# Decoder trunk on one core: sample keys fetched one sample ahead and multiplied on VectorE, the samples' cross scores moved into the first feed-forward

## The chip, the cores and the metric

The kernel runs on one core of a Trainium2 chip. The metric is the device time of one execution in microseconds, from the first to the last instruction with what the launch adds around them. Three runs of the kernel before took 3188.86, 3189.97 and 3193.72 us; their median is 3189.97 us.

## What is computed

One layer of a decoder trunk in float32, for two groups at once: a prompt of 2048 tokens and 8 samples of one token each (model width 1024).

1. Normalise, project to pool, q, k and v; a pooling mixer for one half of the width, differential attention (4 heads, two score maps of 64 dimensions each) for the other half; output projection, added to x.
2. Normalise, cross-attention (4 heads of 256) into 256 memory tokens, added to x.
3. Normalise, feed-forward 1024 to 2 x 2816 with a causal convolution of width 3, silu gate, down to 1024, added to x. Final norm.

The samples attend to caches in place of the prompt. Two pieces of the reference are computed by the lines that change:

```python
# differential attention of a sample: 512 cached keys, found through a page table of 4 pages of 128 rows
past_k = cache_k[l][page_table].reshape(Bs, -1, N_DIFF_HEADS, 2 * DIFF_HD)
s = jnp.einsum('bqhcd,bkhcd->bhcqk', q, k) * (DIFF_HD ** -0.5)
# cross-attention of a sample: its own 256 memory keys, 4 heads of 256
s = jnp.einsum('bqhd,bkhd->bhqk', q, mem_k) * (CROSS_HD ** -0.5)
```

## The kernel before, in words

The prompt is cut into four chunks of 512 tokens, features on the partitions; the 8 sample tokens ride as 8 extra columns of chunk 3. Every product of the prompt is a float32 product made of three matmuls: weight and activation are split into a rounded part (hi, a copy on ScalarE) and a remainder (lo, a subtraction on VectorE), and lo x hi, hi x hi and hi x lo are summed. `split` (L88) and `mm3` (L92) do it for activations, the class `Weight` (L281) for weights: stage 0 loads 512 KB by the SP queue (L291), stage 1 casts `whi` on ScalarE (L294), stage 2 subtracts `wlo` on VectorE (L297).

The order of all work is one list written by hand (L1658 to L1679) that `drive` (L396) walks; each item issues instructions to the engines' in-order queues. An item has a cost (TensorE's share of it) and a latency. `weave(main, extra, lo, hi)` (L337) spreads the items of `extra` by their latencies over the stretch from `lo` to `hi` of the costs of `main`. `look(4, 3, 2)` (L391) lets raw weights run four, casts three and remainders two weights ahead of use. `later(dt, ...)` (L373) holds an epilogue back by so many units of cost.

Tiles come from rings: `H` has 43 buffers of 1060 columns, shared by weights, activations and sample data; `St` has 6 buffers of 536 columns; PSUM has four banks in `PB` and two double banks in `PA`. A transfer into a ring's buffer waits, in its queue, until the last reader of the buffer's old content is done, and what stands behind it in that queue waits too. The SP queue carries the loads of weights and activations and the broadcasts of the samples' queries; the POOL queue carries stores (`ST = G`) and the gathers through the page table.

Two stretches hold what changes.

*First stretch, "stage A"* (L1672): the cross-attention scores of chunk 1 (`sc_[1]`: four heads, matmuls L94 to L96 into S, softmax L1220 to L1228, turned by L1248 into `Ahi`, `Alo`), then the output projection of chunk 2 (`wo[2]`: an item `load` that fetches x and mix and splits mix into `mixhi` and `mixlo`, then eight projections L443). The samples' first attention is woven in from 0 to 0.95: `sample_index`, `sample_rows` (writes the queries to `qs_d`), eight `sample_scores(b)` (L865), `sample_softmax`, `sample_weights`. One `sample_scores(b)` loads the query to all partitions (`qb`, an `St` buffer, SP queue), then twice: two gathers of 128 rows x 512 (L872, POOL queue) into one `kg`, the product kg x qb on GpSimd (L877), and sums over 64 on VectorE (L879) with scale and bias (four small L882 a sample).

*Second stretch, "stage B"* (L1675): the scores of chunk 3 (`sc_[3]`), then its value product (`vo[3]`, L94 to L96 into `vo`). Woven in from 0.3 to 0.95: the list `sc_items`, then `n3[0]`, the feed-forward's norm of chunk 0. `sc_items` is the samples' cross query (`both("q", ...)`, four items of two weights each, L1320), its write to `qcs_d`, eight `sc_scores(b)` (L1344), `sc_softmax`, `sc_weights`. One `sc_scores(b)` broadcasts the query (`qcb`, 512 KB, SP queue), then twice: loads 512 KB of memory keys (`cmk`, L1350), multiplies on GpSimd (L1351), sums over 256 on VectorE (L1352). 

Behind it stands the feed-forward of chunk 0 (`ffn_items(0)`, L1628: 44 up-projections `up`, L429 and L432, of cost 5.3; 88 pieces of the down-projection `down`, L1503, of cost 1.3), with `sc_items2` (the samples' cross values and their output projection) and `n3[1]` woven in. Three more feed-forwards follow, and the final norm.

Of the kernel before, what the change touches and what calls it, by code (L numbers as in the profile page):

```python
# [15 lines left out]
ALU = mybir.AluOpType  # L16
# [4 lines left out]
P = 128  # L21
T = 2048
NS = 8
D = 1024
# [17 lines left out]
PAGES = 4  # L42
# [4 lines left out]
def tile_trunk_step(ctx: ExitStack, tc: tile.TileContext, a, o):  # L47
    nc = tc.nc
    V, S, G, PE, SY = nc.vector, nc.scalar, nc.gpsimd, nc.tensor, nc.sync
# [10 lines left out]
    def H(name, dt=F32):  # L60
        return hp.tile([P, HT], dt, tag="H", name=name)

    def St(name, dt=F32):
        return sp.tile([P, SW], dt, tag="S", name=name)
# [10 lines left out]
    def v3(t, k, n=None):  # L75
        n = n if n is not None else 1024 // k
        return t[:, : k * n].rearrange("p (k n) -> p k n", k=k)
# [7 lines left out]
    def bc(ap, shape, axis):  # L85
        return ap.unsqueeze(axis).broadcast_to(shape)
# [229 lines left out]
    def item(specs, fn, cost=0.0, lat=0.0):  # L316


        return (specs, fn, cost, max(lat, cost, 0.3))
# [17 lines left out]
    def weave(main, extra, lo=0.0, hi=1.0):  # L337

        tm, te = sum(i[2] for i in main) or 1.0, sum(i[3] for i in extra) or 1.0
        out, k, dm, de = [], 0, 0.0, 0.0  # L340
        for i in main:
            out.append(i)
            dm += i[2]
            while k < len(extra) and lo + (hi - lo) * (de / te) <= dm / tm:
                out.append(extra[k])
                de += extra[k][3]
                k += 1
        return out + extra[k:]
# [42 lines left out]
    def look(*n):  # L391
        def fn(_):
            ahead[:] = n
        return item([], fn)
# [455 lines left out]
    idx = cp.tile([P, NS * PAGES], I32, name="idx")  # L850
# [11 lines left out]
        G.memset(coef[0:32], 1.0)  # L862
        V.tensor_copy(coef[32:64], lamv[32:64, 1:2])

    def sample_scores(b):  # L865
        def fn(_):
            qb = St("qb")
            SY.dma_start(qb[:, :512], qs_d[b].partition_broadcast(P))
            for pp in range(2):
                kg = H("kg")  # L870
                for j in range(2):
                    G.indirect_dma_start(  # L872
                        out=kg[:, j * 512:(j + 1) * 512], out_offset=None,
                        in_=a["cache_k"].rearrange("o n s h d -> (o n s) (h d)"),
                        in_offset=bass.IndirectOffsetOnAxis(ap=idx[:, b * PAGES + 2 * pp + j:b * PAGES + 2 * pp + j + 1],
                                                            axis=0))
                G.tensor_tensor(v3(kg, 2), v3(kg, 2), bc(qb[:, :512], [P, 2, 512], 1), ALU.mult)  # L877
                r = St("sr")
                V.tensor_reduce(v3(r, 16, 1), kg[:, :1024].rearrange("p (a d) -> p a d", d=HD), AX.X, ALU.add)  # L879
                r4 = r[:, :16].rearrange("p (g h c) -> p g h c", g=2, h=NH)  # L880
                for c in range(2):
                    V.scalar_tensor_tensor(sal[:, 2 * pp:2 * pp + 2, c, b, :], r4[:, :, :, c], 0.125,  # L882
                                           sbias[:, 2 * pp:2 * pp + 2, :], ALU.mult, ALU.add)
        return fn

    sbias = cp.tile([P, PAGES, NH], F32, name="sbias")

# [104 lines left out]
                     t1.rearrange("p (h b) -> p h b", h=NH))  # L992

    sample_items = [item([], sample_index), item([], sample_rows, 2.0), item([], sample_bias)]
    sample_items += [item([], sample_scores(b), 0, 4.0) for b in range(NS)]
    sample_items += [item([], sample_softmax, 1.0, 14.0), item([], sample_weights, 1.0, 5.0)]
    sample_items2 = in_turn([sample_av(b) for b in range(NS)]) + [item([], sample_o, 0.0, 5.0), item([], sample_o2, 1.0)]

# [342 lines left out]

    scs = cp.tile([P, 2, NS, NH], F32, name="scs")

    def sc_scores(b):  # L1344
        def fn(_):
            qb = H("qcb")
            SY.dma_start(qb[:, :D], qcs_d[b].partition_broadcast(P))
            for i in range(2):
                kk = H("cmk")
                SY.dma_start(kk[:, :D], a["cache_mem_k"][0, b, i * P:(i + 1) * P].rearrange("p h e -> p (h e)"))  # L1350
                G.tensor_tensor(kk[:, :D], kk[:, :D], qb[:, :D], ALU.mult)  # L1351
                V.tensor_reduce(scs[:, i, b, :].unsqueeze(2), kk[:, :D].rearrange("p (h e) -> p h e", h=NH), AX.X,  # L1352
                                ALU.add)
        return fn

    ast = cp.tile([P, 2, NS, 2, NH], F32R, name="ast")
    comb16 = cp.tile([2 * NS, NS], F32, name="comb16")
# [72 lines left out]
        V.tensor_reduce(xs_add.unsqueeze(3), p4, AX.X, ALU.add)  # L1430

    sc_items = both("q", "wq_c", h2st, sc_qwrite) + [item([], lambda _: None, 0, 5.0)]
    sc_items += [item([], sc_scores(b), 0, 5.0) for b in range(NS)] + [item([], sc_softmax, 0.5, 10.0), item([], sc_weights, 0.5, 5.0)]
    sc_items2 = in_turn([sc_av(b) for b in range(NS)])
    sc_items2 += [item([], sc_osplit, 0, 2.0)] + both("o", "wo_c", ost, sc_xadd) + [item([], lambda _: due(flush=True), 0, 3.0)]

# [222 lines left out]
    order = pre[:1] + [item([], vec_load), look(4, 3, 2)] + kv0[:6] + n1[0][0] + kv0[6:] + [item([], vec_turn)]  # L1659
# [8 lines left out]
    wo, n2, sc_, vo, n3 = zip(*p3)  # L1668
# [3 lines left out]
    order += weave(sc_[1] + wo[2], sample_items, 0.0, 0.95)  # L1672
    order += weave(vo[1] + sc_[2][:8], merge(n2[2], sample_items2[:-2]) + sample_items2[-2:], 0.0, 0.55)
    order += sc_[2][8:] + wo[3]
    order += weave(vo[2], n2[3], 0.0, 0.9) + weave(sc_[3] + vo[3], sc_items + n3[0], 0.3, 0.95)  # L1675
    order += weave(ffn_items(0), sc_items2 + n3[1], 0.05, 0.95)
    order += weave(ffn_items(1), final(0) + n3[2], 0.0, 0.95)
    order += weave(ffn_items(2), final(1) + n3[3], 0.0, 0.92)
    order += weave(ffn_items(3), final(2), 0.0, 0.15)  # L1679
# [30 lines left out]
```

## Time and profile before

| | |
|---|---|
| median of three runs | 3189.97 us |
| the profiled execution: its own time | 3193.62 us |
| its span, first to last instruction | 3191.9 us |
| TensorE busy | 3017.0 us, 95% |
| VectorE busy | 2011.8 us, 63% |
| ScalarE busy | 1368.5 us, 43% |
| GpSimd busy | 512.0 us, 16% |
| mean granted TensorE clock | 0.975 of full speed |

Busy times come from the instructions' durations; matmul ends are modelled, so a matmul's duration is longer than the distance to the next one. [...]

### The profile page before, as it was taken

Reading aid. Unit: us, or ns where it says so; the run is one execution under the profiler, and the core shown is the slowest. Engines: PE = TensorE matmul, PEld = TensorE weight load, DVE = VectorE, ACT = ScalarE, POOL = GpSimd, SP = SyncE. Lnnn points to the kernel's source line nnn. Section 1 sums busy time; section 2 is a strip of 40 time slices with the busy share of each in tenths; the row PEclk is TensorE's granted clock in tenths of the full one; section 3 lists DMA queues with packets and bytes.
Section 4 is the critical chain, followed back from the end, with each engine's and each line's share of the span. In section 5 each row is a group of like instructions: output and inputs, shape, how many; then the busy total and the mean of one; then the engine's idle time right before and its main releaser. Section 6 shows DMA issues by size and latency. Waiting matters only on the chain.

```text
span 3191.9 us, 45478 instructions
## 1 busy us (share of the span) xinstructions
PE 3017.0 (95%) x17694; PEld 2612.9 (82%) x17694; DVE 2011.8 (63%) x3248; ACT 1368.5 (43%) x2185; POOL 512.0 (16%) x905
## 2 busy tenths in 40 slices
PE   7999999999999958999599999999999999999998
PEld 6889899788897856798477778888888878899998
DVE  5725654577677655645666767767576667666556
ACT  5525444456655313333244444444344344443342
POOL 0134233211111074400500000000000100010000
PEclk9999999899999988999799999999999999999999
DMA  8556356434433456553744334343324422343321
GB/s 276 180 159 218 113 165 184 139 123 133 143 90 126 153 171 209 169 200 133 303 136 141 132 106 133 121 130 125 99 86 129 169 93 88 99 140 101 97 80 70
DMA packets 378203, 451.98 MB, mean 142 GB/s; under 512 B 18320, under 2 KB 292247, under 8 KB 377971
## 3 DMA queue, kind: packets, MB, share of 16 engines
q1 hardware_dynamic: 336925, 349.29, 34.1%
q0 software_dynamic: 27264, 89.03, 8.1%
q10 hardware_dynamic: 13798, 10.76, 1.1%
q8 instruction: 139, 2.28, 0.3%
q14 instruction: 77, 0.63, 0.1%
HBM read 364.57 MB, written 84.85 MB: 141 GB/s over the span
## 4 chain that ended last, share of the span: by engine, by line
PE 55%; DVE 3%; DMA 2%; issue 1%; ACT 1%; POOL 1%; SPq 0%; DVEq 0%; ACTq 0%; POOLq 0%
PE up L429 20%; PE down L1503 14%; PE up L432 10%; PE wo L443 2%; PE vo L94 1%; PE vo L95 1%; PE vo L96 1%; PE S L95 1%; PE S L96 1%; PE S L94 1%; DVE wlo L297 1%; DMA vg<-in_cache_v_dram,idx 1%; DMA cmk<-in_cache_mem_k_dram 1%; PE sco L1401 0%; DMA qcb<-qcs_d 0%
## 5 line engine op out<-in xcount | busy, mean ns | idle before, releaser
L297 DVE TENSOR_TENSOR wlo<-wraw,whi 128x1024 fp32r<-128x1024 f32 x432 | 530.9, 1242 | 52.5 <-ACT whi L294 51.0
L429 PE MATMUL up<-h3hi,wlo 128*128 128x512 f32 (+1 forms) x1760 | 558.4, 350 | 2.4 <-DVE wlo L297 2.3
L429 PE MATMUL up<-h3hi,whi 128*128 128x512 f32 (+1 forms) x1760 | 557.3, 349 | 0.0
L294 ACT CAST whi<-wraw 128x1024 fp32r<-128x1024 f32 x432 | 443.3, 1048 | 210.6 <-DMA wraw<-in_w_down_dram 101.0
L1503 PE MATMUL down<-act,whi 128*128 128x512 f32 (+1 forms) x1760 | 446.3, 351 | 2.7 <-DVE xf L1510 2.7
L432 PE MATMUL up<-h3lo,whi 128*128 128x512 f32 (+1 forms) x1760 | 357.6, 349 | 0.0
L429 PEld LDWEIGHTS up<-h3hi,wlo 128*128 128x128 f32 x1760 | 306.7, 188 | 49.7 <-DVE wlo L297 2.6
L429 PEld LDWEIGHTS up<-h3hi,whi 128*128 128x128 f32 x1760 | 306.7, 188 | 45.9
L1463 DVE SCALAR_TENSOR_TENSOR cc<-Uf,vec,cc 128x512 f32<-128x512 f32 x176 | 132.1, 750 | 333.1 <-ACT cc L1457 323.3
L1503 PEld LDWEIGHTS down<-act,whi 128*128 128x128 f32 x1760 | 293.5, 188 | 49.3 <-DVE xf L1510 4.6
L432 PEld LDWEIGHTS up<-h3lo,whi 128*128 128x128 f32 x1760 | 285.7, 188 | 46.7
L1456 ACT COPY Uf<-up 128x512 f32<-128x512 f32 (+1 forms) x176 | 103.4, 588 | 483.5 <-PE up L432 483.5
L1503 PE MATMUL down<-act,wlo 128*128 128x512 f32 (+1 forms) x880 | 278.8, 349 | 0.0
L1462 POOL COPY halo<-Uf 128x2 f32<-128x2 f32 x176 | 43.3, 246 | 1363.7 <-ACT Uf L1456 1353.0
L1510 DVE TENSOR_TENSOR xf<-xf,down 128x512 f32<-128x512 f32 (+1 forms) x308 | 206.3, 684 | 48.4 <-PE down L1503 45.8
L1075 ACT ACTIVATE T<-T,mn 128x1024 f32<-128x1024 f32 (+4 forms) x192 | 172.1, 899 | 132.6 <-DVE mn L1068 123.0
L1057 PE MATMUL sc<-K,Q 128*128 128x512 f32 (+5 forms) x640 | 173.2, 388 | 16.5 <-DVE mn L1068 16.2
L1068 DVE CUSTOM_DVE_ANT_0 T<-sc,Dt 128x1024 f32<-128x1024 f32 (+7 forms) x128 | 125.9, 985 | 75.8 <-PE sc L1057 74.2
L1503 PEld LDWEIGHTS down<-act,wlo 128*128 128x128 f32 x880 | 153.7, 188 | 23.6
L443 PE MATMUL z<-h1hi,wlo 128*128 128x512 f32 (+1 forms) x480 | 157.9, 362 | 4.6 <-DVE pps L668 4.4
L443 PE MATMUL z<-h1hi,whi 128*128 128x512 f32 (+1 forms) x480 | 153.3, 352 | 0.0
L1087 POOL TENSOR_SCALAR T<-T,rc 128x1024 f32<-128x1024 f32 (+4 forms) x96 | 91.7, 962 | 370.7 <-DVE rc L1085 206.7
(416 smaller groups left out, 5965.5 us busy)
## 6 DMA issues: line engine op xcount, KB each, us to landing
wraw<-in_w_up_dram SPq DMA_DIRECT2D x176, 512.0 KB
wraw<-in_w_down_dram SPq DMA_DIRECT2D x88, 512.0 KB
wraw<-in_w_in_dram SPq DMA_DIRECT2D x32, 512.0 KB
Q<-q_d SPq DMA_DIRECT2D x64, 256.0 KB
wraw<-in_w_out_dram SPq DMA_DIRECT2D x32, 512.0 KB
wraw<-m_d SPq DMA_DIRECT2D x32, 512.0 KB
wraw<-vo_d SPq DMA_DIRECT2D x32, 512.0 KB
K<-k_d SPq DMA_DIRECT2D x24, 512.0 KB
```

The lines of the kernel that those rows point to most:

```text
L294: S.copy(self.hi[:, :1024], self.raw[:, :1024])
L297: V.tensor_tensor(self.lo[:, :1024], self.raw[:, :1024], f(self.hi[:, :1024]), ALU.subtract)
L429: PE.matmul(out, w[wi][:, kt, :], kslice(hi, kt, c0, n), start=kt == 0 and wi == 1, stop=False)
L432: PE.matmul(out, w[0][:, kt, :], kslice(lo, kt, c0, n), start=False, stop=kt == KT - 1)
L443: PE.matmul(out, w[wi][:, kt, :], kslice(z, kt, c0, n), start=i == 0, stop=i == 3 * KT - 1)
L1057: PE.matmul(ps[:, j * 512:j * 512 + w], v3(Q[c], 2)[:, z, self.t * P:(self.t + 1) * P], K[c][hf][:, c0:c0 + w], start=z == 0, stop=z == 1)
L1068: V.tensor_tensor_reduce(out, pin, din, -SLOPE[self.h], 3.0e38 if hf == 0 else mn[:, 0:1], ALU.add, ALU.min, mn[:, hf:hf + 1])
L1075: S.activation(tg[:, :mg], tg[:, :mg], AF.Exp, bias=mn[:, last:last + 1], scale=-1.0, accum_out=self.l[:, 2 * g + c:2 * g + c + 1])
L1456: S.copy(sv(U[:, 2:2 + w], c), view)
L1463: V.scalar_tensor_tensor(cc[:, :CH], U[:, 1:1 + CH], vc(CWT + FT + nt), cc[:, :CH], ALU.mult, ALU.add)
L1503: PE.matmul(out, ws[p][wi][:, nt, :], act[:, z + c0:z + c0 + n], start=st_ and p == 0, stop=en and p == 1)
L1510: V.tensor_tensor(sv(xx, c), sv(xx, c), view, ALU.add)
```

## The change

- `sample_scores(b)` is cut in two items. `sample_keys(b)` (latency 2) issues the broadcast of the query and all four gathers; `sample_scores(b)` (latency 4) holds the products, now on VectorE, and the sums. `pairs` puts the keys of sample b+1 ahead of the scores of sample b.
- `sc_scores(b)` is cut in the same way into `sc_keys(b)` (latency 1: three loads) and `sc_scores(b)` (latency 5: the products, now on VectorE, and the sums).
- `sc_items` leaves the list woven into `sc_[3] + vo[3]` and goes to the head of the list woven into `ffn_items(0)`, which now starts at 0.02 in place of 0.05. `n3[0]` alone is woven into `sc_[3] + vo[3]`, from 0.4 in place of 0.3.

```diff
+    def sample_keys(b):
         def fn(_):
             qb = St("qb")
             SY.dma_start(qb[:, :512], qs_d[b].partition_broadcast(P))
...
+            kgs = [H("kg") for _ in range(2)]
+            for g in range(PAGES):
+                G.indirect_dma_start(
+                    out=kgs[g // 2][:, (g % 2) * 512:(g % 2 + 1) * 512], out_offset=None,
...
+            skg[b] = qb, kgs
+        return item([], fn, 0, 2.0)
+
+    def sample_scores(b):
+        def fn(_):
+            qb, kgs = skg.pop(b)
+            for pp, kg in enumerate(kgs):
+                V.tensor_tensor(v3(kg, 2), v3(kg, 2), bc(qb[:, :512], [P, 2, 512], 1), ALU.mult)
                 r = St("sr")
                 V.tensor_reduce(v3(r, 16, 1), kg[:, :1024].rearrange("p (a d) -> p a d", d=HD), AX.X, ALU.add)
...
+        return item([], fn, 0, 4.0)
+
+    def pairs(first, then, n, by):
+
+        out = [first(i) for i in range(by)]
+        for i in range(n):
+            out += [first(j) for j in range(i + by, min(i + by + 1, n))] + [then(i)]
+        return out
...
-    sample_items += [item([], sample_scores(b), 0, 4.0) for b in range(NS)]
+    sample_items += pairs(sample_keys, sample_scores, NS, 1)
...
+    def sc_keys(b):
         def fn(_):
             qb = H("qcb")
             SY.dma_start(qb[:, :D], qcs_d[b].partition_broadcast(P))
+            kks = [H("cmk") for _ in range(2)]
             for i in range(2):
...
-                G.tensor_tensor(kk[:, :D], kk[:, :D], qb[:, :D], ALU.mult)
+                SY.dma_start(kks[i][:, :D], a["cache_mem_k"][0, b, i * P:(i + 1) * P].rearrange("p h e -> p (h e)"))
+            skg["c", b] = qb, kks
+        return item([], fn, 0, 1.0)
+
+    def sc_scores(b):
+        def fn(_):
+            qb, kks = skg.pop(("c", b))
+            for i, kk in enumerate(kks):
+                V.tensor_tensor(kk[:, :D], kk[:, :D], qb[:, :D], ALU.mult)
                 V.tensor_reduce(scs[:, i, b, :].unsqueeze(2), kk[:, :D].rearrange("p (h e) -> p h e", h=NH), AX.X,
                                 ALU.add)
-        return fn
+        return item([], fn, 0, 5.0)
...
-    sc_items += [item([], sc_scores(b), 0, 5.0) for b in range(NS)] + [item([], sc_softmax, 0.5, 10.0), item([], sc_weights, 0.5, 5.0)]
+    sc_items += pairs(sc_keys, sc_scores, NS, 1) + [item([], sc_softmax, 0.5, 10.0), item([], sc_weights, 0.5, 5.0)]
...
-    order += weave(vo[2], n2[3], 0.0, 0.9) + weave(sc_[3] + vo[3], sc_items + n3[0], 0.3, 0.95)
-    order += weave(ffn_items(0), sc_items2 + n3[1], 0.05, 0.95)
+    order += weave(vo[2], n2[3], 0.0, 0.9) + weave(sc_[3] + vo[3], n3[0], 0.4, 0.95)
+    order += weave(ffn_items(0), sc_items + sc_items2 + n3[1], 0.02, 0.95)
```

## Rows read from the trace of the kernel before

**Rows 1.** The page: TensorE's busy line, and the chain that ended last by engine.
```profile
PE 3017.0 (95%) x17694; PEld 2612.9 (82%) x17694; DVE 2011.8 (63%) x3248; ACT 1368.5 (43%) x2185; POOL 512.0 (16%) x905
...
PE 55%; DVE 3%; DMA 2%; issue 1%; ACT 1%; POOL 1%; SPq 0%; DVEq 0%; ACTq 0%; POOLq 0%
```

**Rows 2.** Stretches: length, busy of PE, PEld, DVE, ACT, POOL, clock, DMA, GB/s.
```profile
1115.00:1170.50 55.50, 49.41 (x414) 48.46 (x412) 30.72 (x43) 9.66 (x23) 42.22 (x31) 1.00 0.49 152
1170.50:1199.50 29.00, 0.20 (x3) 0.01 (x1) 15.65 (x26) 6.71 (x20) 22.73 (x16) 0.54 0.65 208
1199.50:1258.10 58.60, 53.23 (x223) 42.10 (x224) 33.31 (x49) 17.55 (x25) 15.81 (x11) 0.91 0.60 207
...
1485.80:1543.60 57.80, 56.90 (x469) 53.29 (x468) 28.76 (x31) 22.50 (x47) 3.67 (x4) 1.00 0.50 168
1543.60:1571.30 27.70, 2.99 (x18) 2.38 (x16) 19.78 (x18) 5.96 (x14) 22.26 (x10) 0.59 0.78 317
1571.30:1635.20 63.90, 50.69 (x208) 40.46 (x209) 41.74 (x56) 13.49 (x18) 16.85 (x10) 0.86 0.55 198
1635.20:2010.00 374.80, 371.15 (x1682) 292.53 (x1681) 261.18 (x356) 172.76 (x228) 12.34 (x86) 1.00 0.41 135
```

**Rows 3.** TensorE's waits in stages A and B: total us, times, longest us.
```profile
PE wo L443 <- ACT mixhi L89: 29.3, 2, 28.8
...
PE AT L1248 <- DVE E L1228: 17.5, 1, 17.5
...
PE vo L94 <- DVE Alo L90: 7.8, 1, 7.8
```

**Rows 4.** GpSimd's groups in stage A: count, busy us, mean ns, idle before.
```profile
L877 POOL TENSOR_TENSOR kg<-kg,qb 128x1024 f32<-128x1024 f32 x16 | 38.5, 2409 | 12.7 <-DMA kg<-in_cache_k_dram,idx 10.4 <-issue 2.2
L872 POOL DMA_INDIRECT kg<-in_cache_k_dram,idx x32 | 37.1, 1159 | 8.3 <-issue 7.5
```

**Rows 5.** VectorE's groups in stage A.
```profile
L297 DVE TENSOR_TENSOR wlo<-wraw,whi 128x1024 fp32r<-128x1024 f32 x14 | 21.4, 1554 | 0.8 <-issue 0.8
L879 DVE TENSOR_REDUCE sr<-kg 128x16 f32<-128x1024 f32 x16 | 19.4, 1216 | 32.1 <-POOL kg L877 32.1
```

**Rows 6.** The SP queue's own waits in stage A: total, times, longest.
```profile
SPq L868 <- POOL kg L877: 25.1, 3, 12.0
```

**Rows 7.** The chain in order of time where scores end before wo[3]: start, us.
```profile
1385.97 1.24 DVE mx L1220
...
1391.04 1.64 PE AT L1248 x8
1392.68 46.98 PE wo L443 x384
```

**Rows 8.** VectorE's timeline in stage A, two places: start, us, line, count.
```profile
1156.15 1.20 DVE L297 TENSOR_TENSOR wlo<-wraw,whi 128x1024 fp32r<-128x1024 f32 x1
1157.26 1.22 DVE L1228 TENSOR_TENSOR E<-E,rcx 128x1024 f32<-128x1024 f32 x1
1158.40 1.22 DVE L297 TENSOR_TENSOR wlo<-wraw,whi 128x1024 fp32r<-128x1024 f32 x1
...
1172.54 2.35 DVE L297 TENSOR_TENSOR wlo<-wraw,whi 128x1024 fp32r<-128x1024 f32 x2
```

**Rows 9.** GpSimd's timeline beside the first place of rows 8.
```profile
1157.28 3.16 POOL L872 DMA_INDIRECT kg<-in_cache_k_dram,idx  x1 [0.30 <-issue]
```

**Rows 10.** GpSimd's groups over the whole span: the samples' value gathers.
```profile
L937 POOL DMA_INDIRECT vg<-in_cache_v_dram,idx x32 | 49.5, 1545 | 9.8 <-issue 7.6 <-DMA vg<-in_cache_v_dram,idx 1.2 <-ACT h2sq L227 0.3
```

**Rows 11.** One line of TensorE, vo of chunk 0: ns min/median/max, first and last start.
```profile
L95 PE MATMUL vo<-Ahi,whi x64: 388/392/401, 1067.7 to 1114.8; 128*128 128x512 f32 x64
```

**Rows 12.** The chain in order of time in stage B: start, us, what.
```profile
1514.28 0.94 PE sx L1320 x8
...
1538.41 9.58 DMA qcb<-qcs_d
1548.01 10.06 DMA cmk<-in_cache_mem_k_dram
```

More of the change, by code (lines that the diff above doesn't have):

```diff
@@ L863, in sample_index @@
         V.tensor_copy(coef[32:64], lamv[32:64, 1:2])
-    def sample_scores(b):
+    skg = {}
+    def sample_keys(b):
         def fn(_):
@@ L868, in fn @@
             SY.dma_start(qb[:, :512], qs_d[b].partition_broadcast(P))
[L869 to L877, printed above, removed]
+            kgs = [H("kg") for _ in range(2)]
+            for g in range(PAGES):
+                G.indirect_dma_start(
+                    out=kgs[g // 2][:, (g % 2) * 512:(g % 2 + 1) * 512], out_offset=None,
+                    in_=a["cache_k"].rearrange("o n s h d -> (o n s) (h d)"),
+                    in_offset=bass.IndirectOffsetOnAxis(ap=idx[:, b * PAGES + g:b * PAGES + g + 1], axis=0))
+            skg[b] = qb, kgs
[5 more added lines that the diff above has]
+                V.tensor_tensor(v3(kg, 2), v3(kg, 2), bc(qb[:, :512], [P, 2, 512], 1), ALU.mult)
                 r = St("sr")
@@ L1342, in tile_trunk_step @@
     scs = cp.tile([P, 2, NS, NH], F32, name="scs")
-    def sc_scores(b):
+    def sc_keys(b):
         def fn(_):
@@ L1347, in fn @@
             SY.dma_start(qb[:, :D], qcs_d[b].partition_broadcast(P))
+            kks = [H("cmk") for _ in range(2)]
             for i in range(2):
-                kk = H("cmk")
-                SY.dma_start(kk[:, :D], a["cache_mem_k"][0, b, i * P:(i + 1) * P].rearrange("p h e -> p (h e)"))
-                G.tensor_tensor(kk[:, :D], kk[:, :D], qb[:, :D], ALU.mult)
+                SY.dma_start(kks[i][:, :D], a["cache_mem_k"][0, b, i * P:(i + 1) * P].rearrange("p h e -> p (h e)"))
[6 more added lines that the diff above has]
+                V.tensor_tensor(kk[:, :D], kk[:, :D], qb[:, :D], ALU.mult)
                 V.tensor_reduce(scs[:, i, b, :].unsqueeze(2), kk[:, :D].rearrange("p (h e) -> p h e", h=NH), AX.X,
                                 ALU.add)
-        return fn
+        return item([], fn, 0, 5.0)
     ast = cp.tile([P, 2, NS, 2, NH], F32R, name="ast")
```

## The prediction

> **What bounds the kernel now.** I read the page first. The chain that ended last is mostly TensorE, and VectorE is busy 63% of the span, GpSimd 16% [rows 1]. So the time is TensorE's stream of matmuls plus the holes in it, and an edit of VectorE's or GpSimd's work counts only where it opens or closes a hole. Next I cut the two stages that the change touches into stretches, by the first and last matmul of each line. Stage A (1115.0 to 1258.1, 143.1 us) has a stretch of 29.0 us in which TensorE is busy 0.20 us; behind it the output projection runs 58.6 us at a granted clock of 0.91. Stage B (1485.8 to 1635.2, 149.4 us) has 27.7 us with 2.99 us of TensorE at clock 0.59, and then 63.9 us at 0.86 [rows 2]. The first feed-forward, into which work is moved, has no hole worth naming: 371.15 of 374.8 us busy, VectorE 261.18 of them.
>
> Then TensorE's waits name what ended last. In stage A it is `mixhi` on ScalarE, 28.8 us at once; in stage B the last head's softmax, `E` on VectorE (17.5 us), and then `Alo` (7.8 us) [rows 3]. Neither is slow work of its own. ScalarE and VectorE run their queues in order, and in front of these instructions stand the samples' sums: in stage A VectorE sat 32.1 us waiting for GpSimd's products [rows 5]. GpSimd itself is full there: 38.5 us of products and 37.1 us of gathers, with 21 us of waits before them [rows 4], 96.6 us for eight samples or 12.1 us a sample. The SP queue is held too: the query broadcast of a later sample waits for GpSimd to let go of an `St` buffer, 25.1 us in three waits, and the loads of x and mix stand behind it [rows 6]. GpSimd's product is thus the pace of a stage whose results TensorE needs from other engines.
>
> **Part 1, products to VectorE in stage A.** Removed: 16 GpSimd products of 2.41 us [rows 4]. Added: 16 VectorE products of the same shape; the nearest operation is the weight remainder `wlo`, two float32 inputs of 128x1024, two of them back to back 2.35 us, so 1.18 us each [rows 8], 18.9 us in all. Off the same engine goes a stretching: in stage A `wlo` took 1.554 us on average over 14 [rows 5], 0.37 us over 1.18, which is 5.2 us; where a GpSimd product was running, VectorE's two-input operations ended only after it.
>
> VectorE until `mixhi`: it was busy 30.72 + 15.65 = 46.4 us from 1115.0 to 1199.5 [rows 2], and six samples' sums lie in that. By the spacing (latency 6 a sample; 69.6 in all over 0.95 of a cost of 88.4) again six samples' scores stand ahead of the mix load. So 46.4 + 12 x 1.18 less half of the stretching, 2.6: 58 us. I add 9 us in which it must wait at the start as it does now (transposes of the queries, their write, the first gathers). It gets to the end of the last head's softmax at 1115 + 67 = 1182, and the projection starts about there in place of 1199.5. The projection itself takes 47 us where nothing disturbs it, as wo[3] does [rows 7], in place of 58.6: the end moves from 1258.1 to 1229, **29 us earlier**. VectorE's remaining work in the projection, the 33.31 us of now, fits under 47.
>
> Bounds: TensorE's part of the scores ends at 1170.5 and the softmax behind it takes 7 us (1385.97 to 1392.68 [rows 7]), so the projection can't start before 1177.5 unless the 6.1 us that TensorE idles in the first stretch go as well [rows 2]: 34 to 40 us at best. At the other end stand the gathers. GpSimd now has only these, 4 x (1.159 + 0.30) = 5.8 us a sample at today's mean, well under 12. But one gather took 3.16 us, and it is the one beside three two-input operations in a row on VectorE [rows 8, 9]; the value gathers, beside a busier VectorE, average 1.545 us [rows 10]. At 3.16 + 0.30 four take 13.8 us a sample, more than GpSimd's 12.1 of now, and the stage would lose 14 us. I take 1.545, 7.4 us a sample, nearest in kind (the same instruction from the next stage): eight samples end by 1117 + 59 = 1176, before VectorE is through.
>
> [...]
>
> **Part 2, keys one sample ahead.** The four gathers and the broadcast of sample b+1 stand before the products of sample b. The same 32 gathers and 8 broadcasts are issued. The broadcast now waits for the `St` buffer of a product on VectorE two samples back, no longer for GpSimd, so SP gets to x and mix once the fifth sample is multiplied, before the scores end. One more pair of `H` buffers is held. I cost this at nothing beside part 1; if the ring of 43 has no free buffer, gathers wait and the lead is gone (a rival below).
>
> **Part 3, cross scores out of stage B.** TensorE's own part of the scores stretch is 57.8 us less the samples' query matmuls: 64 at 0.94/8 us [rows 12] are 7.5 us, and about 1.1 us of waits around them, so 49.2. Then the softmax of the last head and its turn: 6.7 us as at wo[3] [rows 7], plus two casts and remainders, 9 us in place of 27.7. Then vo: chunk 0's runs from 1067.7 to 1115.2, 47.5 us [rows 11], in place of 63.9 at clock 0.86. Sum 105.7 against 149.4 [rows 2]. I leave 2 us for the norm `n3[0]`, which is now spread from 0.4 and ends before vo does: **41.5 us earlier**. Bounds: 43.7 if the norm costs nothing; 25 if the gap behind the softmax stays (27.7) and only vo recovers its pace. What is late next is that softmax alone, since nothing stands before `E` any more.
>
> **Part 4, the same work in the feed-forward.** TensorE takes along 7.5 us of query matmuls and about 2 us of small turns: **9.5 us later**, as it has no hole to hide them. VectorE gets 8 x 4 x 1.18 = 38 us and eight weight remainders. The list woven in grows from latency 131 to 207 over 0.93 x 347.6 of cost, so one sample (latency 6) gets about 9.4 us. VectorE's load there is 0.70 today [rows 2], some 0.58 without the value splits, their copies and the norm, which come later in the list (an estimate: 16 x 1.2, 16 x 0.7 and 15 us off the 261): 5.5 us, with 4.7 us for the sample 10.2 in 9.4. It lags by 0.8 us a sample, **6 us** in all; 0 if weights two ahead and four PSUM banks absorb it, 14 if today's full 0.70 stands beside it. Ahead of it, the eight query weights come in 20 us of TensorE's time with ScalarE and VectorE still under it, which I take as nothing. The transfers, 1.5 MB a sample in 9.4 us, are 160 GB/s on top of 135; stage B shows 317 GB/s at a share of 0.78 [rows 2]. The new wait is VectorE's at the head of its queue for `cmk` and `qcb`; behind it stand `wlo` and the additions that free PSUM, for which TensorE waits.
>
> **Sum.** -29 - 41.5 + 9.5 + 6 = -55. The profiled execution's own time is 3193.6 us (span 3191.9): 3138.6. It lies 3.6 us over the median of the runs shown, so in their terms **3135 us**.
>
> **The rivals.**
>
> *Starved gathers.* VectorE, now nearly full, keeps the gathers near 3 us; the stage is paced by GpSimd as before and A gives some 5 us. For it: rows 8 and 9. Against: VectorE then waits for the gather, and the waiting itself leaves GpSimd free; the sums have one input. Time: 3193.6 - 5 - 41.5 + 15.5 - 3.6 = 3159.
>
> *All hidden.* A gives its 40, B 43.7, and the feed-forward absorbs the lag: 3193.6 - 83.7 + 9.5 - 3.6 = 3116. Against: VectorE is the engine in line in both places.
>
> *No lead.* The rings have no free buffers, keys land no earlier than now, A gives nothing, B as forecast: 3193.6 - 41.5 + 15.5 - 3.6 = 3164. The change then doesn't do what it says in A.
>
> *Slower: the head of VectorE's queue in the feed-forward.* If the three loads of a sample go out only when the sample before has let its buffers go, VectorE stands through the transfers, 9.58 and 10.06 us in stage B [rows 12], with `wlo` behind it. A sample then takes 10 + 4.7 + 5.5 = 20 us in place of 9.4, some 84 us for eight, and TensorE starves with it: 3135 - 6 + 84 = 3213. It decides from 8 us a sample on, where 70.5 us of gain are used up by 61 of lag and 9.5 of moved work. For it: in stage B TensorE did starve behind just such waits. Against: loads are issued 9 us ahead on a queue with half the bandwidth free, and the rival needs all eight samples late.
>
> **How the numbers follow.** Forecast 0.52 (own range 3115 to 3152), starved gathers 0.17, all hidden 0.17, no lead 0.06, slower 0.08. The range 3106 to 3176 takes in all but the slower case and some tails. A measurement of this kernel tells 0.2%, about 6 us, from no change. Faster: all cases but the last, less a little that mixtures take, 0.89; same 0.03; slower 0.08.
>
> **What would show it.** After: in stage A the product on VectorE near 1.2 us, gathers near 1.5 us, the wait for `mixhi` under 12 us, stage near 114 us. In stage B a wait for `E` of 5 us, no SP or VectorE wait for `cmk`, 106 to 108 us. In the first feed-forward some 390 us for what was 375, with waits for `wlo` and `xf` of up to 10 us. I am wrong if TensorE waits there for over 30 us, if gathers pass 2.5 us on average, or if stage A's projection starts after 1190.

## The result, and the profile after

The kernel after takes 3144.26 us (median of four runs, 3141.94 to 3150.45). The kernel before, run beside it, takes 3190.67 (3188.86 to 3193.72). The ratio is 0.9857, with a 95% interval of 0.984 to 0.9874: 46 us faster. The prediction was 3135.

The profiled execution of after took 3144.37 us, its span is 3142.6 and its mean granted clock 0.983 (before: 3193.62, 3191.9 and 0.975). On the page, TensorE's busy line answers to [rows 1]:

```profile
PE 3016.3 (96%) x17694; PEld 2609.5 (83%) x17694; DVE 2023.8 (64%) x3280; ACT 1369.2 (44%) x2187; POOL 439.5 (14%) x873
...
PE 60%; DVE 4%; DMA 2%; issue 1%; ACT 1%; POOL 1%; SPq 0%; DVEq 0%; ACTq 0%; POOLq 0%
```

The same number of matmuls, as many busy microseconds, and more of the chain on TensorE: what changed is its idle time, 174.9 us of the span before and 126.3 after. The stretches of [rows 2], cut in after at the same places of the program (length, busy of PE, PEld, DVE, ACT, POOL, granted clock, DMA share, GB/s; the last of them is the first feed-forward):

```profile
1109.90:1162.30 52.40, 50.53 (x414) 49.80 (x412) 42.66 (x62) 13.09 (x34) 38.49 (x34) 0.97 0.78 242
1162.30:1170.50 8.20, 0.00 (x0) 0.00 (x0) 8.20 (x15) 3.57 (x11) 3.76 (x4) 0.66 1.04 373
1170.50:1222.40 51.90, 51.17 (x223) 40.93 (x224) 35.89 (x59) 17.42 (x25) 2.16 (x3) 0.95 0.60 210
1450.70:1498.20 47.50, 47.50 (x403) 47.45 (x402) 20.78 (x26) 14.97 (x37) 0.69 (x1) 1.00 0.43 151
1498.20:1507.30 9.10, 2.96 (x18) 2.64 (x17) 8.86 (x11) 5.23 (x14) 0.00 (x0) 0.76 0.35 140
1507.30:1554.10 46.80, 46.80 (x205) 38.05 (x205) 28.36 (x43) 15.03 (x16) 1.73 (x4) 0.97 0.44 147
1554.10:1962.00 407.90, 391.56 (x1759) 304.19 (x1758) 297.83 (x396) 181.45 (x245) 15.98 (x90) 0.97 0.48 160
```

Against [rows 2]: stage A 143.1 became 112.5 (-30.6), stage B 149.4 became 103.4 (-46), the first feed-forward 374.8 became 407.9 (+33). Stage A also begins 5.1 us earlier. No line of the change stands ahead of it, so this is left out; the profiled execution of before lies 3.0 us over its own median. Between the stages and behind the first feed-forward there is 1 us of difference in all. So the change itself is worth about 44 us in these two executions: 77 gained in two places and 33 given back in a third.

TensorE's waits in stage A (total us, times, longest), for [rows 3]:

```profile
PE wo L443 <- ACT mixhi L89: 9.0, 3, 8.3
```

The 28.8 us for `mixhi` are 8.3. VectorE's and GpSimd's groups in stage A (count, busy us, mean ns, idle before), for [rows 4, 5]:

```profile
L297 DVE TENSOR_TENSOR wlo<-wraw,whi 128x1024 fp32r<-128x1024 f32 x15 | 17.8, 1213 | 1.6 <-ACT whi L294 1.6
L884 DVE TENSOR_TENSOR kg<-kg,qb 128x1024 f32<-128x1024 f32 x16 | 19.3, 1211 | 4.6 <-DMA kg<-in_cache_k_dram,idx 4.6
```
```profile
L873 POOL DMA_INDIRECT kg<-in_cache_k_dram,idx x32 | 39.3, 1228 | 11.3 <-issue 8.2 <-ACT E L1240 1.8 <-DMA kg<-in_cache_k_dram,idx 0.6
```

The product takes 1.211 us on VectorE (2.409 on GpSimd), `wlo` fell from 1.554 to 1.213, and the 32.1 us that VectorE sat waiting for GpSimd are 4.6 us waiting for gathers. What holds `mixhi` now is seen in the timelines of VectorE and ScalarE (start, us, line, what; in brackets the wait before it), and beside them in the chain:

```profile
1165.08 1.20 DVE L1234 TENSOR_REDUCE mx<-S 128x4 f32<-128x1024 f32 x1
1166.21 1.21 DVE L884 TENSOR_TENSOR kg<-kg,qb 128x1024 f32<-128x1024 f32 x1
1167.35 0.15 DVE L1235 TENSOR_SCALAR nbx<-mx 128x4 f32<-128x4 f32 x1
```
```profile
1167.62 0.47 ACT L1240 ACTIVATE E<-S,nbx 128x256 f32<-128x256 f32 x1 [4.61 <-DVE nbx L1235]
...
1169.43 1.05 ACT L89 CAST mixhi<-mixr 128x1024 fp32r<-128x1024 f32 x1
```
```profile
1158.56 10.76 DMA mixr<-mix_d
```

TensorE's scores end at 1162.3, and it starts the projection at 1170.53, behind the first `mixhi`. That cast stands on ScalarE right behind the last head's exponentials, without a wait of its own; these waited 4.61 us for `nbx` on VectorE, where a sample's product stands between `mx` and `nbx`. The mix transfer that the chain shows, sent at 1158.56 behind a query broadcast, ends at 1169.32, within 0.2 us of the exponentials. So the softmax and the load are late together, and which of them alone would keep the hole is not shown. The other three casts do wait for the load, 6.7 us in all, in a stretch with a DMA share of 0.79 to 1.04, and cost TensorE 0.7 us.

The holes of the first feed-forward. TensorE's waits in stage B's gap, and then from 1554 to 1962 (before had 3.6 us in its first feed-forward, in two):

```profile
PE AT L1262 <- DVE E L1242: 6.1, 1, 6.1
...
PE down L1524 <- DVE xf L1531: 7.0, 3, 6.0
PE up L429 <- DVE wlo L297: 6.8, 2, 3.5
```

The chain through the first two holes, in order of time:

```profile
1559.79 3.72 PE up L429 x16
...
1565.38 1.88 PE sx L1334 x16
...
1568.67 1.28 ACT L1497
...
1572.60 6.41 PE up L429 x16
...
1614.48 1.27 PE down L1524 x6
1615.74 9.46 DMA xf<-x_d
...
1626.05 7.25 PE down L1524 x24
```

First hole: the moved query weights (`sx`, 1.88 us of TensorE for two weights' matmuls) use up weights faster than casts and remainders come, and `wlo` stands on VectorE behind a step of the feed-forward (`cc`, L1498) that waits for ScalarE's activation, with a table load of 1.28 us ahead of it (L1497). Sixteen `up` matmuls then take 6.41 us, where sixteen take 3.72 at 1559.79. Second hole: TensorE begins `down` at 1614.48, and the x that `down` is added to is loaded only then. The SP queue shows why: its waits from 1598 to 1620 (total, times, longest), then its timeline (start, us, line, what):

```profile
SPq L291 <- DVE wlo L297: 8.6, 1, 8.6
SPq L1361 <- DMA qcs_d<-qcs: 5.1, 1, 5.1
```
```profile
1613.57 1.11 SPq L1361 DMA_DIRECT2D qcb<-qcs_d  x1
1614.78 0.86 SPq L1364 DMA_DIRECT2D cmk<-in_cache_mem_k_dram  x2
1615.74 3.59 SPq L1466 DMA_DIRECT2D xf<-x_d  x4
```

The queue stood 5.1 us for the write of the samples' query, which the moved broadcast reads, then 8.6 us for a weight's buffer, and then sent that weight and a sample's keys; the x load is behind all of it. Before, it was issued 10 us ahead of the first `down`. Two windows behind the holes (columns as above) show what else they cost:

```profile
1572.00:1579.00 7.00, 6.40 (x17) 5.10 (x18) 5.69 (x6) 3.25 (x4) 0.00 (x0) 0.57 0.69 209
...
1614.00:1634.00 20.00, 14.00 (x55) 10.88 (x54) 18.89 (x23) 6.38 (x8) 0.28 (x2) 0.83 1.00 363
```

The granted clock is 0.57 in the first one and 0.83 in the second. A third hole of 3.3 us, again for `wlo`, ends at 1882.87, and 1880 to 1900 runs at 0.83; before had 2.3 us there, with a granted clock of 1.00 from 1895 to 1915. Over the whole feed-forward 391.56 busy of 407.9 leaves 16.3 us idle, where before had 3.6 (+12.7). Busy time grew by 20.4, of which the moved matmuls are about 10.5 (64 x 1.88/16 = 7.5, 1.8 for the query's turn in the chain, about 1.2 for the softmax's, the last an estimate); the other 10 are what is left, and are read as matmuls at a lower granted clock behind the three holes (the sixteen above alone took 2.7 us more).

### The profile page after: what moved, and what is told of

The parts are those of the page before. It is cut to its first block, busy times and chain, and to the rows that moved or that the text cites. A ratio compares the mean times of both kernels' runs of the same rounds, so it can differ in the third digit from the quotient of the medians.

```text
span 3142.6 us, 45471 instructions
## 1 busy us (share of the span) xinstructions
PE 3016.3 (96%) x17694; PEld 2609.5 (83%) x17694; DVE 2023.8 (64%) x3280; ACT 1369.2 (44%) x2187; POOL 439.5 (14%) x873
## 4 chain that ended last, share of the span: by engine, by line
PE 60%; DVE 4%; DMA 2%; issue 1%; ACT 1%; POOL 1%; SPq 0%; DVEq 0%; ACTq 0%; POOLq 0%
PE up L429 21%; PE down L1524 14%; PE up L432 10%; PE wo L443 4%; PE vo L94 2%; PE vo L95 2%; PE vo L96 2%; PE S L94 1%; PE S L96 1%; PE S L95 1%; DMA vg<-in_cache_v_dram,idx 1%; DVE wlo L297 1%; DMA mixr<-mix_d 1%; PE O L1123 1%; POOL vg L951 1%
## 5 line engine op out<-in xcount | busy, mean ns | idle before, releaser
L297 DVE TENSOR_TENSOR wlo<-wraw,whi 128x1024 fp32r<-128x1024 f32 x432 | 520.4, 1219 | 50.3 <-ACT whi L294 49.6
L1484 DVE SCALAR_TENSOR_TENSOR cc<-Uf,vec,cc 128x512 f32<-128x512 f32 x176 | 132.0, 750 | 328.5 <-ACT cc L1478 324.0
L1082 DVE CUSTOM_DVE_ANT_0 T<-sc,Dt 128x1024 f32<-128x1024 f32 (+7 forms) x128 | 125.8, 985 | 76.2 <-PE sc L1071 74.5
L1123 PE MATMUL O<-V,wT 128*128 128x128 f32 x1088 | 149.2, 278 | 1.8 <-ACT wT L1114 1.3
```

The source lines that it names most:

```text
L297: V.tensor_tensor(self.lo[:, :1024], self.raw[:, :1024], f(self.hi[:, :1024]), ALU.subtract)
L1082: V.tensor_tensor_reduce(out, pin, din, -SLOPE[self.h], 3.0e38 if hf == 0 else mn[:, 0:1], ALU.add, ALU.min, mn[:, hf:hf + 1])
L1123: PE.matmul(O[:, self.t * P:(self.t + 1) * P], self.wt[g][:, (j % 4) * P:(j % 4 + 1) * P], v3(Vt[j // 8], 8)[:, j % 8, :], start=j == 0, s ...
L1484: V.scalar_tensor_tensor(cc[:, :CH], U[:, 1:1 + CH], vc(CWT + FT + nt), cc[:, :CH], ALU.mult, ALU.add)
```

## The experiments

"Before" was run beside each; its medians lay between 3187 and 3192. Stage lengths are from one profiled execution each. Stage A runs from the first matmul of the scores of chunk 1 to the first `vo` behind the projection, stage B from the first of the scores of chunk 3 to the first `up`, the feed-forward from there to GpSimd's first copy of the next one:

| us | stage A | stage B | first feed-forward | median | ratio to before (95%) |
|---|---|---|---|---|---|
| before | 142.7 | 149.6 | 375.4 | 3190.67 | |
| after | 112.1 | 103.2 | 407.9 | 3144.26 | 0.9857 (0.984-0.9874) |
| a_full | 125.8 | 149.0 | 375.8 | 3165.29 | 0.9911 (0.9886-0.9936) |
| a_full2 | 112.1 | 147.9 | 377.4 | 3157.16 | 0.9906 (0.9877-0.9934) |
| a_vec | 133.9 | 148.0 | 377.7 | 3176.95 | 0.9959 (0.9934-0.9984) |
| a_lead | 130.2 | 147.3 | 377.2 | 3180.79 | 0.9969 (0.9955-0.9982) |
| b_stay | 119.3 | 138.4 | 377.1 | 3156.68 | 0.9895 (0.9858-0.9932) |
| b_gps | 112.1 | 103.1 | 415.7 | 3153.61 | 0.989 (0.9873-0.9906) |
| c_open | 112.0 | 103.7 | 405.4 | 3144.41 | 0.986 (0.9844-0.9876) |
| c_none | 111.5 | 103.4 | 404.5 | 3141.73 | 0.9854 (0.9838-0.9871) |
| c_both | 113.0 | 103.1 | 397.6 | 3139.69 | 0.983 (0.9809-0.9851) |
| d_mix12 | 122.6 | 103.0 | 402.4 | 3152.04 | 0.9884 (0.9867-0.99) |
| d_q | 114.2 | 116.8 | 387.1 | 3139.02 | 0.983 (0.981-0.9851) |
| d_spread | 113.4 | 116.9 | 345.2 | 3135.12 | 0.9828 (0.9804-0.9852) |

(So the first two rows differ by up to 0.6 us from the windows above.) How well one profile's length repeats can be read from rows with the same code in a stage: the feed-forward takes 375.4 to 377.7 us in the six in which it is as before, and 405.4 and 402.4 in `c_open` and `d_mix12`.

**Stage A by parts.** `a_full` keeps parts 1 and 2 and puts the cross scores back as they were, `sc_scores` on GpSimd without a lead included:

```diff
-    order += weave(vo[2], n2[3], 0.0, 0.9) + weave(sc_[3] + vo[3], n3[0], 0.4, 0.95)
-    order += weave(ffn_items(0), sc_items + sc_items2 + n3[1], 0.02, 0.95)
+    order += weave(vo[2], n2[3], 0.0, 0.9) + weave(sc_[3] + vo[3], sc_items + n3[0], 0.3, 0.95)
+    order += weave(ffn_items(0), sc_items2 + n3[1], 0.05, 0.95)
```

> Stage A of the change alone (sample keys one ahead, products on VectorE); the cross scores stay in stage B, on GpSimd, as before. If the stages add up: stage A 112 us in place of 143, stage B 149 and the first feed-forward 375 as before, 3160 us. If the gains of the two stages are not independent (the shared rings, the transfers that run ahead), the time is off 3160 by over 6 us.

`a_vec` is `a_full` with the gathers back inside `sample_scores` (no lead; a sample then has latency 4 in the weave in place of 2 + 4, so that its spacing changes too). `a_lead` is `a_full` with the product back on GpSimd:

```diff
-                V.tensor_tensor(v3(kg, 2), v3(kg, 2), bc(qb[:, :512], [P, 2, 512], 1), ALU.mult)
+                G.tensor_tensor(v3(kg, 2), v3(kg, 2), bc(qb[:, :512], [P, 2, 512], 1), ALU.mult)
```

> The kernel before with one word changed: stage A's products on VectorE, gathers and products still in one item. Theory 'product': the gathers run ahead by themselves once no product stands in GpSimd's queue, so this gives what the whole stage A edit gives, stage A 112 to 116 us, 3160 to 3164 us. Rival 'lead': without the keys one sample ahead VectorE waits some 6 us a sample at the head of its queue for the gathers, stage A stays near 140 us, over 3180 us.

> Stage A with the keys one sample ahead, products still on GpSimd; stage B as before. Theory 'product': GpSimd still needs 2 x 2.4 + 4 x 1.3 = 10 us a sample, so the stage loses only the 10 us of waits for gathers: 133 to 143 us, 3180 to 3191 us. Rival 'lead': most of the gain is here, stage A under 120 us, 3165 us.

`a_vec` falls between its two forecasts, `a_lead` at the near end of its first. By the ratios, products alone are worth 13 us (5 to 21), the lead alone 10 (6 to 14), both 28 (20 to 36). Neither alone gives what both give; whether the two add up or help each other these intervals can't tell. The wait that the rival of `a_vec` rests on is not there: VectorE waits for gathers 5.6 us in all, in two waits, and 4.6 in after. With GpSimd still multiplying, the SP queue stays held in `a_lead` (the queue's waits in stage A), which answers to [rows 6]:

```profile
SPq L870 <- POOL kg L884: 25.4, 2, 13.2
```

`a_full` left a puzzle: the same code of stage A in the same order as in after, and 13.7 us longer. TensorE's waits there ("issue": the engine waited for nothing that the profile shows):

```profile
PE S L94 <- issue: 4.5, 6, 1.8
PE S L95 <- issue: 3.8, 5, 1.1
PE S L96 <- issue: 3.3, 4, 1.1
```

Fifteen holes of 0.4 to 1.8 us ahead of single matmuls, 11.6 us in all. `a_full2` is the same code once more, to see whether they belong to it:

> a_full once more, the same code. Its stage A took 125.8 us in the profile, 14 us over that of the whole change, with the same instructions in the same order up to the end of the stage; TensorE stood there in holes of about 1 us that no wait explains. Theory 'by chance': such holes come and go between executions, a new profile's stage A and its own time move together, stage A about 112 us plus the profiled time less 3162 us. Rival 'by the program': what comes later in the program changes stage A; 125 us again whatever the time.

They don't belong to every execution: stage A took 112.1 us with no such hole, and this kernel's six runs reach from 3156.64 to 3177.88, the first four alone from 3157.89. `a_full2` ran on another chip than `a_full`, so its profile alone can't tell the execution from the chip. The holes also show in `a_vec` (10.5 us), `b_stay` (4.9) and `d_q` (2.8). A trace of them is in `c_both` (0.5), and the scores of stage A have none in the other runs, `a_lead` among them, which ran on the chip of `a_full`, `a_vec` and `b_stay`. They come where gathers fill the DMA engines (`a_full` has 10 us at a share of 0.99 there), yet after has such a stretch without these holes (0.94 from 1134 to 1144), and the instruction queues moved 5 packets from 1120 to 1165 in `a_full` and 4 each in `a_full2` and after. Their cause is open.

**What the move is worth.** `b_stay` is the whole change, with `sc_items` left in stage B (new form: keys ahead, products on VectorE). Its edit is the two `order` lines shown above alone.

> The change, but the cross scores stay woven into stage B (from 0.3), with the keys one ahead and the products on VectorE; the first feed-forward is as before. Theory 'move': stage B's hole comes from VectorE's queue with the samples' sums and from 20 MB of transfers in it, so without the move stage B gains only about 10 us (139 us), and the time is near 3150 us. Rival 'product': the hole came from GpSimd's pace, so VectorE's products alone close it; stage B about 115 us, the first feed-forward stays at 375 us, 3125 us, below the change.

Stage B took 138.4 us for 103.2, the first feed-forward 377.1 for 407.9: the move gains 35 and gives 31 back, a net of 4 in profiled stages. The medians differ by 12, with 4.9 us of issue holes on `b_stay`'s side, but the intervals of the two ratios overlap (0.9858 to 0.9932, 0.984 to 0.9874): that the move pays is not clear of noise. TensorE's waits in its stage B show that the gap behind the softmax is not GpSimd's alone:

```profile
PE AT L1262 <- DVE E L1242: 22.3, 1, 22.3
```

With the products on VectorE, these stand in front of `E` (five products and five sums between the last head's `mx` at 1524.74 and `E` at 1537.31), in place of waits for GpSimd (20.7 us in before's stage B, none here).

**Which engine in the feed-forward.** `b_gps` is after with the cross products on GpSimd:

```diff
-                V.tensor_tensor(kk[:, :D], kk[:, :D], qb[:, :D], ALU.mult)
+                G.tensor_tensor(kk[:, :D], kk[:, :D], qb[:, :D], ALU.mult)
```

> The change with the cross products back on GpSimd, inside the first feed-forward: VectorE has 19 us less there, GpSimd is idle in that stretch otherwise. Theory 'VectorE lags': the feed-forward's 408 us falls to about 396 us, 3133 us. Rival 'queue order': its holes come from loads and casts that stand behind the samples' in their queues; 405 to 412 us, 3142 to 3148 us. GpSimd's products may also hold up two-input operations of VectorE.

Slower by 7.8 us in that section, outside both forecasts, and 7.2 of it TensorE's idle time (TensorE's waits, VectorE's group over it, and the `wlo` in front of the longest of these waits):

```profile
PE down L1524 <- DVE wlo L297: 8.2, 4, 4.2
```
```profile
L297 DVE TENSOR_TENSOR wlo<-wraw,whi 128x1024 fp32r<-128x1024 f32 x74 | 95.3, 1309 | 3.1 <-ACT whi L294 2.7
```
```profile
1664.58 3.36 DVE L297 TENSOR_TENSOR wlo<-wraw,whi 128x1024 fp32r<-128x1024 f32 x1
```

In after `wlo` takes 1.216 us in the same section, 1.309 here, and `cc` (L1484) 0.747 and 0.870: taking 19 us of products off VectorE lengthened these and left its busy time as it was (297.99 us for 297.83). VectorE also stood 7.5 us at the head of its queue for GpSimd's products, so the 7.8 us are not the stretching alone. Stage A shows the same from the other side: `wlo`'s 1.554 us of [rows 5], beside GpSimd's products, are 1.213 in after without them.

**The hole at the first `down`.** Two theories: the late x load, or VectorE's backlog of two samples' products ahead of `xf`. `c_open` moves the load ahead of the feed-forward; `c_none` leaves the products and sums out and puts two copies of four columns in their place, so that the samples' cross scores are not computed:

```diff
+    order += [item([], ffn_open(0))] + weave(ffn_items(0), sc_items + sc_items2 + n3[1], 0.02, 0.95)
...
-                if g == 1:
+                if g == 1 and c:
```

> The change with one item moved: the four loads of x for the first feed-forward's additions are issued before its first up-projection, ahead of the samples' key loads. Theory 'queue order': the 6.0 us hole before the first down-projection's additions goes, with the granted clock of 0.83 behind it; the feed-forward takes 398 us, 3134 us. Rival 'VectorE lags': the hole moves to the next addition or weight, 405 us or more, 3142 us.

```diff
-                V.tensor_tensor(kk[:, :D], kk[:, :D], qb[:, :D], ALU.mult)
...
+                V.tensor_copy(scs[:, i, b, :], kk[:, :NH])
+                V.tensor_copy(kk[:, :NH], qb[:, :NH])
```

> The change without the cross products and their sums (the keys are still loaded; the samples' cross scores are not computed): 38 us of VectorE less in the first feed-forward. Theory 'VectorE lags': it falls to about 390 us (375 and the moved 10 us and some), 3127 us. Theory 'queue order': the hole before the additions of x stays, 398 to 403 us, 3135 to 3140 us.

Neither closed it: 5.3 us remain in the one, 5.6 in the other. VectorE in `c_open`, from its timeline (start, us, line):

```profile
1619.64 1.22 DVE L1372 TENSOR_TENSOR cmk<-cmk,qcb 128x1024 f32<-128x1024 f32 x1
1620.78 1.22 DVE L297 TENSOR_TENSOR wlo<-wraw,whi 128x1024 fp32r<-128x1024 f32 x1
...
1624.17 1.27 DVE L1531 TENSOR_TENSOR xf<-xf,down 128x512 f32<-128x512 f32 x2
```

x is there, but a full queue stands in front of `xf`. And in `c_none`:

```profile
1623.90 0.17 DVE L1372 COPY scs<-cmk 128x4 f32<-128x4 f32 x1 [3.39 <-DMA cmk<-in_cache_mem_k_dram]
...
1626.53 1.29 DVE L1530 TENSOR_TENSOR xf<-xf,down 128x512 f32<-128x512 f32 x2 [0.98 <-DMA xf<-x_d]
```

VectorE is free, and waits for keys at the head of its queue, then for x. (In `c_none` and `c_both` lines behind the products have a number lower by one.) So `c_both` makes both edits:

> c_open and c_none together: x loaded ahead, and the cross products and sums left out (the samples' cross scores are not computed). Theory 'two covers': the hole before the first down-projection has two causes side by side, the late loads of x and VectorE's backlog of two samples' products, each of which alone keeps 5 us of it; with both away it closes, and the first feed-forward falls from 404.5 to about 398 us, 3135 us. Rival 'third cause': VectorE's wait for the keys' transfers at the head of its queue holds it as well; 403 us, 3141 us.

The hole is gone, and the section is 397.6 us:

```profile
PE down L1523 <- DVE xf L1530: 0.9, 2, 0.6
```

Two causes side by side, each enough. `c_none`, 38 us less of VectorE's work, had given 3.4 us; with the load early the same edit gives 7.8 (405.4 to 397.6). The 3.4 and the 2.5 of `c_open` are no more than what one profile's length repeats to; the 10.3 us of `c_both` are more, and the holes themselves are plain: 6.0 us in after, 5.3 in `c_open`, 5.6 in `c_none`, 0.6 in `c_both`. The medians of the four can't be told apart.

**Versions.** `d_mix12` is `c_open` with the item that loads and splits mix four items earlier, inside the scores, against the 8.3 us wait of stage A:

```diff
-    order += weave(sc_[1] + wo[2], sample_items, 0.0, 0.95)
+    order += weave(sc_[1][:12] + wo[2][:1] + sc_[1][12:] + wo[2][1:], sample_items, 0.0, 0.95)
```

> The loads of x as in c_open and, in stage A, the item that loads x and mix for the projection moved four items ahead, before the last head's scores. If stage A's 8.3 us wait for mixhi is the transfer of mix, issued late on the SP queue, it falls to the 3 to 4 us of the softmax and the cast, stage A to 107 us, 3130 us with c_open's gain. If the sixteen buffers of the load are not free earlier, the loads wait in the SP queue, weights behind them, and stage A stays at 112 us or grows.

Ten us slower in stage A. The wait for `mixhi` is gone, and in its place TensorE waits

```profile
PE wo L443 <- DVE wlo L297: 17.9, 1, 17.9
```

for the projection's weights. Their casts stand on ScalarE behind those of mix, which now wait for the transfers of mix at the head of the queue (ScalarE's waits):

```profile
ACT mixhi L89 <- DMA mixr<-mix_d: 14.3, 3, 5.3
```

The last of them starts at 1176.73, the weights' `whi` right behind it at 1177.69. On VectorE `wlo` (1178.95) stands behind `mixlo` in the same way, and TensorE goes on at 1180.32. The item moves the splits of mix in the engines' queues together with its loads, so the edit doesn't test the loads alone.

`d_q` is `c_open` with the query projection left in stage B, `d_spread` is `d_q` with `sc_items2` (the samples' cross values) moved on into the second feed-forward:

```diff
+    sc_q = both("q", "wq_c", h2st, sc_qwrite) + [item([], lambda _: None, 0, 5.0)]
+    sc_items = pairs(sc_keys, sc_scores, NS, 1) + [item([], sc_softmax, 0.5, 10.0), item([], sc_weights, 0.5, 5.0)]
...
+    order += weave(vo[2], n2[3], 0.0, 0.9) + weave(sc_[3] + vo[3], sc_q + n3[0], 0.3, 0.95)
+    order += [item([], ffn_open(0))] + weave(ffn_items(0), sc_items + n3[1], 0.02, 0.95)
+    order += weave(ffn_items(1), final(0) + sc_items2 + n3[2], 0.0, 0.95)
```

(`d_q` keeps `sc_items2` in the second of these lines.)

> c_open, with the samples' query projection (four matmul groups, eight weights) left in stage B as before; only the scores and their loads move. The query's matmuls cost TensorE the same 10 us in either place, but in the feed-forward they also opened a 3.5 us hole for a weight's remainder with a lower clock behind it. So stage B 112 us in place of 103, the feed-forward 390 in place of 405, 3137 us. Rival: the eight weights come between the last head's softmax operations in stage B and give the hole back; 3144 us or more.

> d_q, and the samples' cross values (sc_items2) go one feed-forward later, behind the final norm of chunk 0, so that one sample's products get about 19 units of cost in place of 9. Theory: the holes of the first feed-forward come from too much of the samples' loads and sums in a short stretch; then the first feed-forward holds no wait over 2 us, the second gets 25 us of TensorE's work from the first, and the sum of stage B and both falls by 17 us against c_open: 3127 us. Rival: the second feed-forward gets the holes in turn (two chunks' final tiles and the values share the ring); 3137 us or more.

With the query projection out of the feed-forward its first hole is gone: the one wait for `wlo` left in `d_q` is the 2.3 us that before had too. From stage B's start to the last transposes (`cvp`, L1635, some 31 us before the end) `c_open` takes 1658.8 us, `d_q` 1653.0, `d_spread` 1644.3. The profile of `d_q` is its slowest run and that of `d_spread` its fastest (3143.89 and 3125.64 us), so the 8.7 us between these two are not shown. TensorE's waits in `d_spread` from stage B to the second feed-forward:

```profile
PE vo L94 <- DVE Alo L90: 5.3, 1, 5.3
PE AT L1262 <- DVE E L1242: 4.2, 1, 4.2
PE down L1524 <- DVE xf L1531: 0.9, 2, 0.7
```

Nothing of the first feed-forward's holes is left; the second has two, of 1.9 and 1.7 us. `d_spread` has the lowest median, 3135.12 us (3125.64 to 3143.46); its ratio can't be told from that of `d_q`, and its interval still overlaps the one of after (0.984 to 0.9852).

## Why the prediction was right, and where it wasn't

**Bound.** Right: 17694 matmuls before and after. In the two profiled executions TensorE's idle time fell by 48.6 us and its busy time by 0.7.

**Part 1.** Right. The product took 1.211 us (1.18), `wlo`'s stretching went (1.554 to 1.213 us), the projection began 60.6 us after the stage's start (67), and stage A gained 30.6 (29). The path was the one worked out, VectorE's queue up to the last head's softmax, with six samples' products (12) ahead of the first `mixhi`; that the mix transfer ended at the same moment was not foreseen. Two terms were off and cancelled, which is luck: VectorE was busy 49.8 us up to there, not 58, so that the projection began 6.4 us sooner, and it then took 51.9 us for 47. The 47 were read where no turn of a last head stands in the projection and the granted clock was 0.98; here the turn does, so do two short waits for `mixhi` (0.7 us), and the first 10 us ran at a granted clock of 0.76. That two-input operations ended only after a running GpSimd product is what the long ones show: before's longest `wlo`, 3.74 us from 1139.84, ended 1.10 us after the product of 1140.12 to 1142.48, and an `E` of 2.25 us from 1198.75 ended 1.09 us after the one of 1197.55 to 1199.91. It doesn't hold for all: an addition to `x` (L1201) that reads `wo` from PSUM took 0.68 us at 1216.04, inside the product of 1215.86 to 1218.32.

**Starved gathers.** False: their mean was 1.228 us (1.545 taken, 1.159 before). The long gather does exist, once, and beside the same thing as in [rows 8, 9]. GpSimd's timeline, and VectorE's beside it:

```profile
1146.96 3.41 POOL L873 DMA_INDIRECT kg<-in_cache_k_dram,idx  x1 [0.30 <-issue]
```
```profile
1146.06 2.35 DVE L297 TENSOR_TENSOR wlo<-wraw,whi 128x1024 fp32r<-128x1024 f32 x2
1148.34 1.21 DVE L884 TENSOR_TENSOR kg<-kg,qb 128x1024 f32<-128x1024 f32 x1
1149.47 1.28 DVE L90 TENSOR_TENSOR Alo<-AT,Ahi 128x512 fp32r<-128x512 f32 x2
```

It ended at 1150.37. The three operations up to 1149.55 have both inputs in SBUF, the two `Alo` read one (`AT`) from PSUM; the gather ended 0.82 us after the last of the three, and the one of [rows 8, 9] 0.82 us after the last of its three. Two of before's value gathers (L937) took 5.02 us each, from 1302.88 and 1311.55, and ended 0.83 and 0.82 us after the last of such a row (1307.07 and 1315.75). The other thirty-one of after took 1.92 us at most, 0.94 at best; those over 1.1 us all ended 0.8 to 0.9 us after such an operation that ran when they began. The mean stayed at 1.228, so it cost little here.

**Part 2.** No wait of TensorE for its transfers shows but the 0.7 us for `mixhi`. "Nothing beside part 1" undersold it: without the lead (`a_vec`) the products gave 13 us (5 to 21), not 29. Part of this is `a_vec`'s 10.5 us of issue holes; beside `a_full`, which has 11.6, its stage A is 8.1 us longer. What the lead saves there stays open: it is not VectorE's wait for keys (5.6 us without it, 4.6 with it), and the spacing changed too.

**Part 3.** Right in each term: scores 47.5 (49.2), gap 9.1 (9), vo 46.8 (47.5). The 2 us left for the norm were not needed: 46 for 41.5.

**Part 4.** This is the step that failed. The moved matmuls were sized right (10.5 for 9.5, 1.2 of it an estimate). The lag, put at 6 us with 14 as a bound, was 23: 12.7 of holes and some 10 that are read as a lower granted clock behind them (0.57 and 0.83), for which the sum has no term. So the section took 407.9 us and not some 390. The reason given was a part only. It treated VectorE's throughput, 10.2 us of work in 9.4; all of that work is worth 3.4 us in `c_none` and 7.8 with the x load early, near the 6 but a third of the 23. Three points of the order cost the time: the query weights, "which I take as nothing" (a hole of 3.5 us and the matmuls at 6.41 us for 3.72 behind it); the x load of the first `down`, which the SP queue sent late; and the samples' products that pile up in front of the first `xf`. The third hole, at 1882.87, stays without an account. The transfers were put at 160 + 135 GB/s on average, while the twenty microseconds in which they decide ran at 363 GB/s and a share of 1.00.

**The slower rival.** Its mechanism is there in small: one wait of 3.4 us for `cmk` in `c_none` (the row at 1623.90). In after VectorE shows no wait for `cmk`: keys one sample ahead were enough.

**The sum.** Against the forecast A was 1.6 us better, B 4.5 better and the feed-forward 17.6 worse: 11.5 us less gain by stages, 9 by the medians. The time lay inside the range because the gain of 77 us was sized right to 6, not because the loss was.

## What to carry to other kernels

A move out of a starved stage is worth what the stage gains less what the receiving stage has no holes to hide: here 35 against 31 by stages, a gain that the times don't show clear of noise. When costing the receiving side, don't divide work by room: go through the moved list instruction by instruction, see which load or remainder of the host's own each one is issued ahead of, and look for the first place where the host needs that. An item moved in the order takes its casts and remainders along, and they can hold the queues where it lands (`d_mix12`). A hole with two sufficient causes doesn't close by removing either, so take both away before calling one innocent.

## What the runs showed that was not expected

- The same program took 3156.64 to 3177.88 us in six runs; its profile at 3177.88 has 11.6 us of TensorE holes behind nothing that it shows, and the one at 3157.69, on another chip, none. Where an experiment is judged by a stage's length, such holes have to be read off first.
- Products taken off VectorE and given to GpSimd (16 of 1.216 us) in `b_gps` left VectorE as busy as before and the section 7.8 us longer, as `wlo` went from 1.216 to 1.309 and `cc` (L1484) from 0.747 to 0.870 us.
- A gather's 0.95 us on GpSimd became 3.16 and 5.02 us in before and 3.41 in after, beside a row of VectorE operations with two inputs in SBUF, and each time ended 0.82 or 0.83 us after the last of them.
- GpSimd's products took 2.667 us in `b_gps`'s first feed-forward on average, for 2.409 in [rows 4], while VectorE's sums, of one input, stayed at 1.21.
